# A hybrid decoder step on one core: another order of the filler blocks around the four chunks of a scan

## The chip, the cores and the metric

The kernel runs on one core of a Trainium2 chip. The metric is device time in microseconds (us) of one execution. The engines are named as in the profile: PE (TensorE, matmuls), ACT (ScalarE), DVE (VectorE), POOL (GpSimd), SP (SyncE, which issues most DMAs).

## The reference, cut to what matters

One decoder layer is computed for a prompt (512 tokens) and a sample group (8 requests of 4 tokens). Only the pieces that the change touches are shown: the modulation rows, the pooled cache rows, the input projection and the scan in four chunks of 128 tokens.

```python
def adaln_mods(c, w_ada, b_ada):
    m = (jax.nn.silu(c) @ w_ada + b_ada)[:, None, :]        # (1024) @ (1024, 6144)
    return jnp.split(m, 6, axis=-1)

def compress(rows, w_pos):                                   # pooled cache rows, 32 to 1
    b, l, g, d = rows.shape
    return jnp.einsum('bcjgd,j->bcgd', rows.reshape(b, l // CMP_BLOCK, CMP_BLOCK, g, d), w_pos)

rows = cache_cmp[layer, page_table].reshape(bd, PAST_LEN, 2, N_KV, HEAD_DIM)
kcmp = rmsnorm(compress(rows[:, :, 0], w_pos_k), g_k_cmp)
vcmp = compress(rows[:, :, 1], w_pos_v)

u = h @ w_in                                                 # (512+32, 1024) @ (1024, 2592)

def step(h, inp):                                            # one chunk of the scan
    xc, dtc, bc, cc = inp
    acs = jnp.cumsum(dtc * a, axis=1)
    seg = acs[:, :, None, :] - acs[:, None, :, :]
    decay = jnp.where(causal, jnp.exp(jnp.where(causal, seg, 0.0)), 0.0)
    cb = jnp.einsum('blhn,bshn->blsh', cc, bc)
    y_diag = jnp.einsum('blsh,bsh,bshp->blhp', cb * decay, dtc, xc)
    y_off = jnp.einsum('blhn,bhpn,blh->blhp', cc, h, jnp.exp(acs))
    w_end = jnp.exp(acs[:, -1:, :] - acs) * dtc
    h_new = jnp.exp(acs[:, -1])[:, :, None, None] * h + jnp.einsum('bsh,bshn,bshp->bhpn', w_end, bc, xc)
    return h_new, y_diag + y_off
```

## The kernel before

The program has three parts: projections and scan (up to about 258 us of the profile), attention, and the mixture of experts. The change touches the first part alone.

The steps of that part are written in an order given by the string `ORDER`. `C`, `z`, `q` and `B` are four projections of the normalised input by column blocks of `w_in` (weights wC, wF, wA, wB). Each splits its float32 weight into a high and a low part, k by k for the 8 blocks of 128 rows (`split_w`: ACT casts `wh` at L334, DVE subtracts `wl` at L335), and takes 12 products of 512 columns per k into four accumulators (tile `acc`); 16 small products per half of the weight are for the samples. Two pairs of wh and wl exist, so a projection's first two k can be split, and their 24 products issued, ahead of time. `c0` to `c3` are the four chunks of the scan (`ssd_chunk`), `p` prepares them, `e` finishes the state. A chunk is a chain over the engines: four transposes (L635), a copy of them (tile xt), small products with masks (UT, LT, ones), an exponential (L661, tile dec), a DVE product (L664), the products xt by dec, twice over for two groups of heads, then the state update (xdw by bt).

Between these stand sixteen filler blocks, which depend on none of them: eight `pool_batch` (pool0 to pool7; two 1 MB gathers from the paged cache, 32 products listed as 64) and eight `ada_block` (ada4 to ada11; a 1024 by 512 block of w_ada in two loads of 1 MB, 32 products listed as 64 and four with the bias listed as 8). They are taken in turn from one list: pool0, ada4, pool1, ada5 and so on to pool7, ada11.

```python
fillers = [f for n in range(8) for f in ((pool_batch, n), (ada_block, n + 4))]
...
BETWEEN = dict(C={3: (fill,), 6: (fill,)}, z={1: (fill,), 5: (fill,)}, q={1: (fill,), 5: (fill,)},
               B={1: (fill,), 3: (fill,), 5: (fill,)})
...
for step in ORDER.split():
    if step[0] == "f":
        fill(int(step[1:]))
    elif step[0] == "c":
        ssd_chunk(int(step[1:]))
    else:
        steps[step]()
```

One filler stands ahead of `ORDER`; a projection runs two or three between its k (after k=1, for instance); `f1` in `ORDER` runs one. What a filler and a projection put on PE is tied into one chain by `in_turn`, so PE takes those products in the order written. The chunks are outside that chain: a scheduler places their instructions among the others when the program is built, and on the chip every engine runs its instructions in that fixed order.

All big loads of the part (weights and gathers, 1 MB each) go through a ring of seven tiles (`SLOT`, pool `st`). A load waits until the tile that it is given has been read for the last time. SP's and POOL's queues are in order, so a load that waits holds up what is behind it.

Behind the part, attention begins with the transposes of the split queries (L913, tile qhl), which PE has right behind ada11; their copies (L100 on DVE, L102 on ACT, tile QT) follow a DVE chain that ends projection B (`k_side`, L563 to L568). The line of most matmuls is that of the helper, L92.

Of the kernel before, what the change touches and what calls it, by code (L numbers as in the profile page):

```python
# [22 lines left out]
TS = 4  # L23
NS = NB * TS
NE = 16
ORDER = "C p z c0 c1 q c2 f1 f1 c3 e B f1 f1 f1 f1"
WB = 6
XAT = 4
LA = 4
# [21 lines left out]
def hybrid_step(ctx: ExitStack, tc: tile.TileContext, a, o):  # L51
# [699 lines left out]
    steps = dict(C=proj_c, z=proj_z, p=ssd_prep, q=proj_q, B=proj_b, e=ssd_end)  # L751
    for step in ORDER.split():
        if step[0] == "f":
# [1422 lines left out]
```

## Time and profile before

| | |
|---|---|
| median of 3 runs | 783.35 us (783.32 to 785.89) |
| the profiled execution's own time | 787.62 us |
| its span, first to last instruction | 785.9 us |
| mean granted TensorE clock in it | 0.938 of full speed |
| PE busy | 709.3 us (90%) |
| DVE busy | 501.2 us (64%) |
| ACT busy | 355.2 us (45%) |
| POOL busy | 151.6 us (19%) |

Times in the trace are us from the span's start. An instruction's duration includes its pipeline, so durations overlap, and what a block costs in a row of blocks is the distance from its start to the next one's. A bracket behind a row is the idle time of its engine ahead of it and what ended that. PEclk is the granted clock of a stretch: 1.00 is 2.4 GHz, 0.50 is 1.2 GHz, and what lies between is a mixture.

### The profile page before, as it was taken

The page shows a single profiled execution, that of the slowest core. Times are in us where ns is not written, and L with a number is a line of the kernel's source. Part 1 is how long each engine was busy: PE and PEld are TensorE (multiplying, and loading weights), DVE is VectorE, ACT ScalarE, POOL GpSimd, SP SyncE. Part 2 cuts the span into 40 slices and gives each one's busy share as a digit, 9 for nine tenths or more (in the row PEclk, how much of TensorE's full clock was granted, in tenths as well). Part 3 has the DMA queues.
Part 4 walks back from the last instruction along what each step waited for, and adds up shares of the span by engine and source line. Part 5 has one row for each costly group of instructions (what it writes and reads, how often), then busy time and mean ns, then how long its engine had stood idle before and what let it go on. Part 6 is the DMA issues. An engine that isn't in the chain of part 4 may idle for free. (4 is left out here: it accounts for less than half of the span.)

```text
span 785.9 us, 14689 instructions
## 1 busy us (share of the span) xinstructions
PE 709.3 (90%) x5565; PEld 511.7 (65%) x5565; DVE 501.2 (64%) x1333; ACT 355.2 (45%) x813; POOL 151.6 (19%) x169
## 2 busy tenths in 40 slices
PE   4999999898999578998989999899668999999993
PEld 3667877676777355665647756687655766767562
DVE  5633692524644767554557555878986888877773
ACT  3423444515233333364434435613433766677661
POOL 1103012121321421010111200020131232233221
PEclk9999999889899879699999889999868999999997
DMA  8964895144559634423445041988767899997311
GB/s 286 355 187 131 289 330 193 58 162 161 214 191 346 253 143 172 149 81 134 164 158 219 2 108 23 360 267 286 290 253 282 270 333 335 334 329 256 86 25 23
DMA packets 67094, 161.86 MB, mean 206 GB/s; under 512 B 19005, under 2 KB 31238, under 8 KB 60622
## 3 DMA queue, kind: packets, MB, share of 16 engines
q1 hardware_dynamic: 56798, 115.54, 42.3%
q0 software_dynamic: 10224, 45.37, 17.5%
q8 instruction: 44, 0.72, 0.4%
q14 instruction: 28, 0.23, 0.1%
HBM read 153.48 MB, written 20.74 MB: 222 GB/s over the span
## 5 line engine op out<-in xcount | busy, mean ns | idle before, releaser
L92 PE MATMUL acc<-wh,hH 128*128 128x512 f32 (+1 forms) x128 | 48.9, 382 | 0.5 <-issue 0.5
L92 PE MATMUL acc<-wl,hH 128*128 128x512 f32 (+1 forms) x128 | 47.3, 370 | 0.0
L92 PE MATMUL acc<-wh,hL 128*128 128x512 f32 (+1 forms) x128 | 47.1, 368 | 0.0
L817 ACT ACTIVATE psb<-s,amx 128x128 f32<-128x128 f32 (+3 forms) x64 | 33.7, 528 | 27.4 <-DVE amx L815 24.3
L92 PE MATMUL acc<-gu,XF 128*128 128x512 f32 x88 | 46.1, 606 | 0.0
L92 PE MATMUL acc<-wh,XH 128*128 128x512 f32 x68 | 44.7, 657 | 0.4 <-ACT XH L1942 0.4
L815 DVE TENSOR_REDUCE amx<-s 128x1 f32<-128x128 f32 (+3 forms) x64 | 30.9, 484 | 17.3 <-PE s L92 17.3
L92 PE MATMUL ps<-wada,scT 128*32 128x128 f32 x768 | 38.0, 301 | 4.1 <-DMA wada<-in_w_ada 3.0
L92 PE MATMUL s<-KT,QT 128*128 128x384 f32 (+3 forms) x128 | 39.3, 392 | 1.3 <-DVE qa L838 0.8
L335 DVE TENSOR_TENSOR wl<-dn,wh 128x512 fp32r<-128x512 f32 x52 | 34.0, 686 | 7.0 <-ACT wh L334 6.9
L92 PEld LDWEIGHTS ps<-wada,scT 128*32 128x32 f32 x768 | 30.6, 122 | 10.3 <-issue 3.6
L1047 POOL DMA_INDIRECT gsel<-in_cache_sel,idx x16 | 20.6, 1289 | 84.3 <-PE smo L92 72.6
L334 ACT CAST wh<-dn 128x512 fp32r<-128x512 f32 x52 | 30.9, 619 | 12.9 <-PE acc L92 11.2
L820 PE MATMUL pt<-ident,psb 128*128 128x128 f32 x160 | 33.3, 308 | 3.3 <-ACT psb L817 3.3
L1991 POOL DMA_INDIRECT out_y_prompt<-yo,gi x13 | 21.4, 1646 | 74.8 <-DVE yo L1985 20.1
L335 DVE TENSOR_TENSOR wl<-gu,wh 128x512 fp32r<-128x512 f32 x44 | 29.5, 685 | 8.4 <-ACT wh L334 7.6
L92 PE MATMUL acc<-wh,HH 128*128 128x512 f32 x68 | 32.3, 478 | 1.6 <-ACT HH L1974 1.2
L334 ACT CAST wh<-gu 128x512 fp32r<-128x512 f32 x44 | 26.1, 619 | 15.8 <-PE acc L92 10.8
L92 PE MATMUL smo<-kt,Qb 128*32 128x512 f32 x80 | 29.6, 614 | 2.3 <-DVE kt L100 2.3
L102 ACT COPY kt<-sm 128x512 f32<-128x512 f32 x32 | 18.5, 584 | 27.6 <-PE sm L1023 24.0
L1985 DVE TENSOR_TENSOR yo<-acc,M 128x512 f32<-128x512 f32 x34 | 23.1, 686 | 11.5 <-PE acc L92 9.1
L92 PE MATMUL acc<-wl,HH 128*128 128x512 f32 x68 | 28.6, 421 | 0.0
(788 smaller groups left out, 1902.9 us busy)
## 6 DMA issues: line engine op xcount, KB each, us to landing
wada<-in_w_ada SPq DMA_DIRECT2D x24, 1024.0 KB
dn<-in_w_down SPq DMA_DIRECT2D x12, 1024.0 KB
gu<-in_w_gate SPq DMA_DIRECT2D x21, 512.0 KB
gu<-in_w_up SPq DMA_DIRECT2D x21, 512.0 KB
gux<-in_w_gate SPq DMA_DIRECT2D x11, 512.0 KB
gux<-in_w_up SPq DMA_DIRECT2D x11, 512.0 KB
wt<-in_cache_win SPq DMA_DIRECT2D x4, 1024.0 KB
wout<-in_w_out SPq DMA_DIRECT2D x4, 1024.0 KB
```

What stands on the lines that cost most here:

```text
L92: T.matmul(out, lhsT, rhs, start=start, stop=stop)
L102: S.copy(out, in_)
L334: S.copy(wh[:, 0:n], w)
L335: (eng or V).tensor_sub(wl[:, 0:n], w, wh[:, 0:n].bitcast(F32))
L815: V.tensor_reduce(mx, ps[:, 0:n], axis=AX.X, op=OP.max, negate=True)
L817: S.activation(pb[:, 0:n], ps[:, 0:n], AF.Exp, bias=mx, accum_out=sm[:, h:h + 1])
L820: T.transpose(pt[:, c * P:(c + 1) * P], pb[:, c * P:(c + 1) * P], ident)
L1047: G.indirect_dma_start(out=t.rearrange("p r c -> p (r c)"), out_offset=None, in_=sel_rows, in_offset=bass.IndirectOffsetOnAxis(ap=idx[:, 2 ...
L1985: V.tensor_tensor(yo[:, cols], po, M5[:, cols], op=OP.mult)
L1991: G.indirect_dma_start(out=y_p, out_offset=bass.IndirectOffsetOnAxis(ap=gi, axis=0), in_=yo, in_offset=None, bounds_check=511, oob_is_err= ...
```

## The change

The string that orders the steps is rewritten. Nothing else in the source changes, and the same sixteen fillers run.

```diff
-ORDER = "C p z c0 c1 q c2 f1 f1 c3 e B f1 f1 f1 f1"
+ORDER = "C p z c0 f1 c1 f1 q c2 f1 f1 c3 f1 e B f1"
```

| place | fillers before | fillers now |
|---|---|---|
| ahead, in C, in z | pool0; ada4, pool1; ada5, pool2 | the same |
| behind c0 | none | ada6 |
| behind c1 | none | pool3 |
| in q | ada6, pool3 | ada7, pool4 |
| behind c2 | ada7, pool4 | ada8, pool5 |
| behind c3 | none | ada9 |
| in B | ada8, pool5, ada9 | pool6, ada10, pool7 |
| behind B | pool6, ada10, pool7, ada11 | ada11 |

Since projection q is tied behind pool3 now, and projection B behind ada9, their products can no longer be placed among those of c1 and c3. PE's order shows it. The columns are line, operation, output and inputs, shape, and a count where equal instructions follow each other; wada is ada's weight, xx the conv output, wh, wl, hH and hL the parts of a projection's operands.

PE before, where c0 ends and c1 begins (first row: c0's state update; L635: c1's transposes):

```order
L92 MATMUL ps_1612<-xdw_1610,bt_1546 64x256 x2
L92 MATMUL ps_1557<-xt_1534,dec_1571 128x64
L635 MATMUL ps_1623<-ident,xx_815 128x128 x3
L92 MATMUL ps_1557<-xt_1534,dec_1571 128x64 x2
L635 MATMUL ps_1623<-ident,xx_815 128x128
L92 MATMUL acc_1724<-wh_1729,hH 128x512
L92 MATMUL acc_1724<-wl_1730,hH 128x512
L92 MATMUL acc_1724<-wh_1729,hL 128x512
```

PE now at the same place:

```order
L92 MATMUL ps_1612<-xdw_1610,bt_1546 64x256 x2
L92 MATMUL ps_1557<-xt_1534,dec_1571 128x64
L92 MATMUL ps_1626<-wada_1622,scT_89 32x128 x3
L92 MATMUL ps_1557<-xt_1534,dec_1571 128x64 x2
L92 MATMUL ps_1626<-wada_1622,scT_89 32x128 x13
L92 MATMUL ps_1581<-UT,lh_1588 128x128
L92 MATMUL ps_1626<-wada_1624,scT_89 32x128
L92 MATMUL ps_1581<-UT,lh_1591 128x128
L92 MATMUL ps_1626<-wada_1624,scT_89 32x128 x15
L92 MATMUL ps_1626<-bada_98,e_16_138 32x128 x4
L635 MATMUL ps_1665<-ident,xx_815 128x128 x4
L638 MATMUL ps_1671<-ident,xx_815 128x128
```

All 24 products of q's k=0 and k=1 stood among c1's rows; now ada6 stands at c0's end, c1's rows follow each other with nothing between, then come pool3 and those 24 products.

PE before, at the start of c3:

```order
L635 MATMUL ps_2187<-ident,xx_815 128x128 x4
L638 MATMUL ps_2193<-ident,xx_815 128x128
L92 MATMUL ps_2193<-dta_907,UT 128x8
L92 MATMUL ps_2193<-dta_907,LT 128x8
L92 MATMUL ps_2193<-dta_907,ones 128x8
L92 MATMUL ps_2203<-xx_815 128x128
L92 MATMUL acc_2317<-wh_2322,hH 128x512
L92 MATMUL acc_2317<-wl_2323,hH 128x512
```

PE now at the start of c3:

```order
L635 MATMUL ps_2267<-ident,xx_815 128x128 x4
L638 MATMUL ps_2273<-ident,xx_815 128x128
L92 MATMUL ps_2273<-dta_907,UT 128x8
L92 MATMUL ps_2273<-dta_907,LT 128x8
L92 MATMUL ps_2273<-dta_907,ones 128x8
L92 MATMUL ps_2283<-xx_815 128x128
L92 MATMUL ps_2286<-xx_815 128x128
L92 MATMUL ps_2290<-UT,lh_2291 128x128
L92 MATMUL ps_2290<-UT,lh_2294 128x128
```

Here too 24 products (B's k=0 and k=1) stood within the chunk; now they stand behind c3, ada9 and the state's transposes.

PE before, the end of the part (pool6, ada10 and pool7 stand ahead of the first row, behind B's last product):

```order
L92 MATMUL ps_2744<-gcmp_2742,PW_837 32x128
L92 MATMUL ps_2782<-wada_2778,scT_89 32x128 x16
L92 MATMUL ps_2782<-wada_2780,scT_89 32x128 x16
L92 MATMUL ps_2782<-bada_98,e_16_138 32x128 x4
L913 MATMUL s_2916<-ident,qhl_2913 128x128 x4
```

PE now, from B's last product on (x4k by Wp are B's own small products):

```order
L92 MATMUL acc_2442<-wh_2690,hL 128x512
L92 MATMUL ps_2730<-x4k_846,Wp_840 16x128
L92 MATMUL ps_2782<-wada_2778,scT_89 32x128 x10
L92 MATMUL ps_2730<-x4k_846,Wp_840 16x128
L92 MATMUL ps_2782<-wada_2778,scT_89 32x128 x2
L92 MATMUL ps_2730<-x4k_846,Wp_840 16x128
L92 MATMUL ps_2782<-wada_2778,scT_89 32x128 x4
L92 MATMUL ps_2782<-wada_2780,scT_89 32x128
L92 MATMUL ps_2730<-x4k_846,Wp_840 16x128 x5
L92 MATMUL ps_2782<-wada_2780,scT_89 32x128 x15
L92 MATMUL ps_2782<-bada_98,e_16_138 32x128 x4
L913 MATMUL s_2916<-ident,qhl_2913 128x128 x4
```

Of four blocks behind B one is left. The ring moves too: ada11's second load took the tile of pool6's first gather, which PE read behind B; now it takes that of wB's first half, which is read in the middle of B. wA's halves, which had tiles that came free during C and z, now take those of pool2's gathers; wB's first half, which had one that came free with pool3, now takes that of wA's second half.

On ACT, both of the early wB casts stand ahead of c2's last exponential (L661) now; before, one of them stood well ahead of it, in front of c2's first exponential.

## Rows read from the trace of the kernel before

**Rows 1.** The page's head: span and busy time.

```profile
span 785.9 us, 14689 instructions
PE 709.3 (90%) x5565; PEld 511.7 (65%) x5565; DVE 501.2 (64%) x1333; ACT 355.2 (45%) x813; POOL 151.6 (19%) x169
```

**Rows 2.** Busy time by stretch of the first part (us, each engine's busy time).

```profile
139.30:159.70 20.40, 17.62 (x101) 14.27 (x100) 10.78 (x25) 8.54 (x22) 3.74 (x3) 0.84 0.08 30
...
203.50:219.70 16.20, 13.98 (x87) 10.97 (x83) 9.97 (x26) 5.21 (x14) 3.40 (x4) 1.00 0.56 215
...
222.40:246.10 23.70, 23.61 (x276) 18.56 (x272) 5.78 (x19) 9.15 (x24) 5.18 (x6) 1.00 0.91 310
246.10:258.40 12.30, 9.87 (x289) 8.69 (x288) 7.72 (x26) 4.20 (x14) 2.04 (x7) 1.00 0.78 271
258.40:280.00 21.60, 12.29 (x77) 8.84 (x70) 20.10 (x68) 8.73 (x21) 11.51 (x19) 0.83 0.80 298
```

**Rows 3.** Timeline of PE, the end of c1 and ada6 (start, duration, ...).

```profile
151.87 0.43 PE L92 MATMUL ps<-xt,dec 128*128 128x64 f32 x2 [2.00 <-DVE dec L664]
152.14 0.66 PE L92 MATMUL ps<-UT,lh 128*128 128x128 f32 x4
...
159.67 3.64 PE L92 MATMUL ps<-wada,scT 128*32 128x128 f32 x64
163.24 0.51 PE L92 MATMUL ps<-bada,e 12*32 12x128 f32 x8
```

**Rows 4.** Windows of acc's products on PE: time, busy, count, granted clock.

```profile
163.70:169.30 5.60, 5.60 (x24) 1.00 0.98 345
```

**Rows 5.** Timeline of PE, the end of c3 and ada8.

```profile
211.92 0.61 PE L92 MATMUL ps<-UT,lh 128*128 128x128 f32 x4
213.96 0.43 PE L92 MATMUL ps<-xt,dec 128*128 128x64 f32 x2 [1.44 <-DVE dec L664]
214.24 0.66 PE L92 MATMUL ps<-UT,lh 128*128 128x128 f32 x4
...
219.15 0.60 PE L711 MATMUL ps<-ident,ST 128*64 128x128 f32 x4
220.16 1.96 PE L92 MATMUL ps<-wada,scT 128*32 128x128 f32 x64 [0.42 <-DVE ts L671]
```

**Rows 6.** PE by windows of 2 us: busy, count, granted clock, DMA.

```profile
152.00:154.00 2.00, 2.00 (x13) 0.81 0.00 0
...
162.00:164.00 2.00, 2.00 (x37) 0.63 0.54 103
...
192.00:194.00 2.00, 0.87 (x5) 1.00 0.00 1
194.00:196.00 2.00, 1.05 (x4) 0.55 0.00 0
...
212.00:214.00 2.00, 0.56 (x6) 1.00 0.40 157
```

**Rows 7.** Timeline of DVE at the start of c3.

```profile
204.06 2.50 DVE L734 TENSOR_TENSOR qa<-qa,rsq_zq 128x512 f32<-128x512 f32 x4
206.48 0.68 DVE L100 COPY xt<-ps 128x512 f32<-128x512 f32 x1
```

**Rows 8.** Timeline of PE: pool4 and ada11.

```profile
201.64 1.95 PE L92 MATMUL ps<-gcmp,PW 128*32 128x128 f32 x64
203.52 0.66 PE L635 MATMUL ps<-ident,xx 128*128 128x128 f32 x4
...
257.09 1.08 PE L92 MATMUL ps<-wada,scT 128*32 128x128 f32 x32 [2.43 <-DMA wada<-in_w_ada]
```

**Rows 9.** Timeline of DVE from B's last norm to the first QT copy.

```profile
251.78 0.76 DVE L568 TENSOR_TENSOR selo<-selo,rsq_zk 128x256 f32<-128x256 f32 x2
...
259.58 0.69 DVE L100 CAST QT<-s 128x512 fp32r<-128x512 f32 x1 [4.36 <-PE s L913]
```

**Rows 10.** Timeline of ACT in c2.

```profile
186.14 0.62 ACT L334 CAST wh<-wB 128x512 fp32r<-128x512 f32 x1 [2.26 <-DMA wB<-in_w_in]
...
194.21 0.60 ACT L661 ACTIVATE dec<-ps 128x512 f32<-128x512 f32 x1
```

## The prediction

> **What bounds the kernel now.** I read the page's head first. PE is busy 709.3 of 785.9 us [rows 1], so PE's own work and its idle time make the time; no block is dropped, and a gain can only come from PE's waits or its clock. Then the windows, stretch by stretch. In c1 (139.30 to 159.70) PE is idle for 2.8 us, in c3 (203.50 to 219.70) for 2.2, in B for 0.1, and behind B (246.10 to 258.40) for 2.4. From 258.40 on DVE is the bound, with 20.10 of 21.60 us [rows 2]. The timeline shows the waits: 2.00 us at 151.87 and 1.44 at 213.96, both for dec of DVE [rows 3, 5], and 2.43 at 257.09 for ada11's second load [rows 8]. DVE begins attention's copies at 259.58 after 4.36 us of idle time, though its own chain of B ended at 252.54 [rows 9]. The windows of 2 us show the clock: it falls in 152:154, after c1's wait, and returns in 162:164; it falls again in 194:196, after c2's waits; in c3 it stays at 1.00 [rows 6].
>
> What must be compared is therefore the stretch from c0's end (139.3) to DVE's first QT copy (259.6): 120.3 us. Ahead of it the two orders are the same, and behind it too.
>
> **Before, in five pieces.** (1) c1, 24 products of q, ada6: 139.3 to 163.7, 24.4 us [rows 2, 4]. (2) The rest of q, c2, ada7, pool4: 163.7 to 203.5, 39.8 us [rows 4, 8]. (3) c3, 24 products of B, the state's transposes, ada8: to 222.4, 18.9 us [rows 2, 5]. (4) B's other 72 products and its samples, pool5, ada9: to 246.1, 23.7 us [rows 2]. (5) pool6, ada10, pool7, ada11 and the way to the QT copy: 13.5 us [rows 2, 9].
>
> **Prices.** 24 products of 512 columns take 5.6 us [rows 4]. A pool block takes 1.9 us (201.64 to 203.52) [rows 8]. An ada block takes 2.24 us at 2.4 GHz (220.16 to 222.4) [rows 2, 5], but ada6, which met the lower clock, took 4.0 (159.67 to 163.7) [rows 3, 4]: 1.8 more. The second half of a chunk took 4.91 us at full clock in c3 (214.24 to 219.15) [rows 5] and 7.53 in c1 (152.14 to 159.67) [rows 3]: 2.6 more. A chunk that loses the clock at its middle thus costs 2.6 + 1.8 = 4.4 us with the block behind it.
>
> **The change, piece by piece, at full clock.**
>
> *Piece 1.* ada6 moves ahead of c1, pool3 and ada7 come behind it, and q's 24 products leave c1's rows for a place behind pool3. c1 alone: the stretch of 20.4 us, less 5.6 for the products, less 2.6 since it ran half at the lower clock: 12.2 us. This takes it that the products covered none of c1's waits; had they covered waits all along, c1 alone would keep 17.8. I take 12.2, since PE was idle only 2.8 of the 20.4 us: the products were mostly work to be done, not cover. Sum: 12.2 + 5.6 + ada6 2.24 + pool3 1.88 + ada7 2.24 = 24.2, against 24.4.
>
> *Piece 2.* It has a block of each kind one number on, at the same price. wB's first half now takes the tile of wA's second half, which PE reads to the end of q (about 186), so it lands later than before, when a cast at 186.14 already waited 2.26 us for it [rows 10]. Both early casts and a scaling now stand ahead of c2's last exponential (194.21 [rows 10]): two casts of 0.6 and a wait. wA's halves, too, come later now, behind pool2's reads, and hold ACT a little in q. Hidden if ACT has slack, at most the 2.26 of the wait seen; I take 1.0: 40.8.
>
> *Piece 3.* B's 24 products leave c3, and ada9 comes behind it. c3 alone, step by step: its xt copy ends 3.6 us after its transposes start (203.52 [rows 8], 206.48 + 0.68 [rows 7]), because DVE works at L734 until then; some 1.9 us of short steps follow (an estimate: copies of 0.7 and small products of 0.6, as in these rows); then 7.2 us from the last group's UT products at 211.92 to the transposes of the state at 219.15 [rows 5]. That is 12.7, between 10.05 (219.15 - 203.5 less 5.6: products never cover) and 15.65 (they always do). Sum: 12.7 + ada9 2.24 + 0.42 for the wait ahead of it [rows 5] + 0.6 transposes + 5.6 = 21.5, against 18.9; the ada block that ended the piece is still in it.
>
> *Piece 4.* Three blocks instead of two: 23.7 + 1.9 = 25.6. Their DVE and ACT copies have room (5.78 and 9.15 of 23.7 us [rows 2]).
>
> *Piece 5.* One ada block remains and stands among B's last products, with its loads into tiles that are free long before, so the 2.43 us of waiting go. What is left is the DVE chain: 252.54 - 246.1 = 6.4, and 0.2 to the copy; ada11's 2.24 us lie beneath it. 6.6 against 13.5. Were that chain not the bound, the floor is about 3 us (ada11 and the transposes); were the samples' work to delay it, 8.
>
> Sum: 24.2 + 40.8 + 21.5 + 25.6 + 6.6 = 118.7 against 120.3, **-1.6 us** at full clock. The tail gives 6.9, and 5.3 goes back, since blocks that stood behind B must run somewhere.
>
> The loads that are issued earlier don't collide: the DMA share is 0.00 where c1 and c2 wait [rows 6]. SP's and POOL's queues keep the order of their loads with the blocks; each block's tiles come free at least a chunk ahead of its use. What a late one costs is shown by ada11: 2.43 [rows 8].
>
> **Why the blocks do not fill the chunks' waits.** PE idled 2.00 us at 151.87 [rows 3], though ada6's products, whose loads had landed (DMA share 0.00 there [rows 6]), came next but for c1's own rows. A block behind a chunk runs behind it. The Trainium skill says so too ("TensorE: Matmul & The Clock Gate", Step-by-step: what each phase is for): matmuls stay in program order, and only weight loads are pulled ahead; the trace agrees. What did fill waits before, 24 products each in c1 and in c3, is what the change takes out.
>
> **The clock.** c1 and c3 now run bare from end to end, as only the last part of each did. c1 before fell after one wait of 2.00; c2 after 0.67 and 1.41 with a few products between (PE busy 0.87 and 1.05 of two times 2 us); c3 stood 1.44 and stayed at 1.00 [rows 3, 5, 6]. Bare c3 has a wait of over 2 us at its start (copy at 206.48, behind L734) and further ones of about 1.3 and 1.1, so I expect it to fall, like c1 before. Bare c1 has no L734 ahead of its copy; its waits, about 1.3 and 1.4 with products between, look like c3's tail, and I expect it to hold, with little margin. One fall is +4.4.
>
> **Forecast.** One of the two chunks, likelier c3, drops to 1.2 GHz: -1.6 + 4.4 = **+2.8 us**. The profiled execution took 787.62 us, 4.3 over the median of 783.35; I add the difference to both: 790.4 for a profile like it, and 786.1 at the median.
>
> **Rivals.**
> - *Both fall (slower).* c1's bare waits are long enough as well. For it speaks c2, which fell on no more; against it c3's tail. -1.6 + 8.8 = +7.2: 790.5. It decides whether PEclk drops in the middle of c1.
> - *Neither falls (faster).* The blocks just ahead of c1 and c3 keep PE busy until the chunk, and the waits stay short: -1.6, 781.8; with the tail at its floor or c3 at its lower bound, down to 779. The Trainium skill's rule ("TensorE: Matmul & The Clock Gate", What's actually happening) is that the clock falls after an idle stretch and that sustained work brings it back; chunks with products between their waits might hold by it, and the sum would be this one. Against it stands c2 at 0.55 in 194:196 after waits of 0.67 and 1.41 [rows 6].
> - *The blocks do cover the waits.* PE would get back the 2.0 and 1.4 us of waiting and the clock besides (4.4), with the tail's gain: -6 to -8, about 776. The order speaks against it: no block's row stands within c1 or c3.
> - *Bare chunks are much longer* (17.8 and 15.65, the upper bounds): about +8 over the sum at full clock, and a fall is then near certain: 793 or more. PE's idle time of 2.8 and 2.2 us before speaks against it.
>
> **How the numbers follow.** One falls 0.44, both 0.26, neither 0.17, the blocks cover 0.05, long chunks 0.08. The time predicted is 786.1. 0.5% of 783.35 is 3.9 us, about what a measurement of this kernel can tell from no change: faster is under 779.4, slower over 787.3. Faster holds the cover case and half of neither, whose bounds reach below: 0.14. Slower holds both, long chunks, and a small part of one-falls, whose piece 2 may cost 1.3 more: 0.38. The same: 0.48. The range runs from 780 to 791: below it lies the cover case and a little of neither, above it the long chunks and a little of both. The likeliest case's own range is 784 to 788.
>
> **What the changed profile would show.** Piece 5 is right if DVE's first QT copy comes within 7 us of B's last product, with no DMA wait at ada11. Piece 1: c1 from transposes to pool3 in 12 us, PEclk 1.00 throughout. Piece 3: a wait of 2 to 3 us behind c3's transposes, PEclk 0.5 in c3's second half, ada9 at nearly 4 us. Piece 2: ACT waits for wB ahead of c2's last exponential. The prediction is wrong if c3 keeps 1.00, if c1 loses it, or if PE waits for a DMA at ada6, pool3 or ada9.

## The result: slower by 0.9%, and the profile after

| | before | after |
|---|---|---|
| median, measured together | 785.89 us (9 runs) | 792.33 us (9 runs) |
| ratio, 95% interval | | 1.0091 (1.0062 to 1.0121) |
| profiled execution, own time | 787.62 us | 797.4 us |
| its span | 785.9 us | 795.7 us |

The ratio is 7 us of 786, beside a forecast of +2.8. It is the number of the rival in which both chunks lose the clock (+7.2). The time itself, 792.33 us, lies above the forecast 786.1 and its range to 791; 2.5 us of that is the kernel before, which was 783.35 us when the forecast was added to it and 785.89 here. Executions more than 1.5% above the fastest of their kernel (two of the kernel before, one of the kernel with a block within c1 and c3) are left out of the ratios.

The page's head after, beside [rows 1]: PE is busy 7.3 us longer with the same 5565 matmuls, so they ran slower.

```profile
span 795.7 us, 14695 instructions
PE 716.6 (90%) x5565; PEld 517.8 (65%) x5565; DVE 502.1 (63%) x1333; ACT 355.9 (45%) x813; POOL 150.3 (19%) x169
```

PE by windows of 2 us after, beside [rows 6] (time, busy, count, granted clock, DMA share, GB/s). The first group is c1 and pool3, the second c2's end, the third c3 and ada9.

```profile
146.00:148.00 2.00, 2.00 (x15) 1.00 1.04 303
148.00:150.00 2.00, 1.94 (x9) 0.57 0.93 393
150.00:152.00 2.00, 0.78 (x4) 0.50 0.05 21
...
164.00:166.00 2.00, 2.00 (x13) 0.66 0.25 26
...
202.00:204.00 2.00, 0.00 (x0) 0.73 0.00 0
...
216.00:218.00 2.00, 1.34 (x6) 0.64 0.96 389
218.00:220.00 2.00, 1.26 (x6) 0.50 1.08 440
...
230.00:232.00 2.00, 2.00 (x42) 0.95 0.47 109
```

c1 falls to 1.2 GHz at about 148, 3 us after its first row, and returns at about 165. Before, it fell 14 us after its first row (139.25 to 153) and was back after 10. c3, which held 1.00 before, is at 0.50 from about 217 to 230. c2 falls as it did before.

PE's timeline after, c1 (beside [rows 3]).

```profile
140.49 0.42 PE L92 MATMUL ps<-wada,scT 128*32 128x128 f32 x6
...
144.94 0.66 PE L635 MATMUL ps<-ident,xx 128*128 128x128 f32 x4
...
151.79 0.69 PE L92 MATMUL ps<-xt,dec 128*128 128x64 f32 x2 [1.22 <-DVE dec L664]
...
157.80 1.12 PE L92 MATMUL ps<-xdw,bt 128*64 128x256 f32 x4 [0.78 <-ACT dec L661]
...
160.75 3.64 PE L92 MATMUL ps<-gcmp,PW 128*32 128x128 f32 x64
164.32 0.80 PE L92 MATMUL acc<-wh,hH 128*128 128x512 f32 x1
```

The waits named are short, 1.22 and 0.78, and the clock had fallen before the first of them began (150.57). The loss is in what runs: pool3 takes 3.57 us (160.75 to 164.32) where a pool block at full clock took 1.9 [rows 8].

PE's timeline after, c3 and what follows (beside [rows 5]).

```profile
212.53 0.66 PE L635 MATMUL ps<-ident,xx 128*128 128x128 f32 x4
...
215.44 0.71 PE L92 MATMUL ps<-UT,lh 128*128 128x128 f32 x4 [1.05 <-DVE xt L100]
...
218.74 0.69 PE L92 MATMUL ps<-xt,dec 128*128 128x64 f32 x2 [1.07 <-DVE dec L664]
...
227.71 3.15 PE L92 MATMUL ps<-wada,scT 128*32 128x128 f32 x64
230.78 0.42 PE L92 MATMUL ps<-bada,e 12*32 12x128 f32 x8
```

DVE's timeline after, from B's last norm to the first QT copy (beside [rows 9]).

```profile
268.05 0.78 DVE L568 TENSOR_TENSOR selo<-selo,rsq_zk 128x256 f32<-128x256 f32 x2
...
269.03 0.67 DVE L100 CAST QT<-s 128x512 fp32r<-128x512 f32 x1
```

DVE no longer waits for PE there: the 4.36 us of idle time are gone, and the tail does what was forecast. The row behind B's last product starts at 262.3, and the copy came 6.7 us after that.

### The profile page after: what moved, and what is told of

The parts are those of the page before. It is cut to its first block, busy times and chain, and to the rows that moved or that the text cites. A ratio compares the mean times of both kernels' runs of the same rounds, so it can differ in the third digit from the quotient of the medians.

```text
span 795.7 us, 14695 instructions
## 1 busy us (share of the span) xinstructions
PE 716.6 (90%) x5565; PEld 517.8 (65%) x5565; DVE 502.1 (63%) x1333; ACT 355.9 (45%) x813; POOL 150.3 (19%) x169
## 5 line engine op out<-in xcount | busy, mean ns | idle before, releaser
L92 PE MATMUL ps<-wada,scT 128*32 128x128 f32 x768 | 39.7, 299 | 0.6 <-DVE rsq_yxs L113 0.3
L92 PE MATMUL s<-KT,QT 128*128 128x384 f32 (+3 forms) x128 | 37.6, 379 | 2.2 <-DVE qa L838 1.2
L820 PE MATMUL pt<-ident,psb 128*128 128x128 f32 x160 | 31.1, 295 | 1.8 <-ACT psb L817 1.4
L504 POOL DMA_INDIRECT gcmp<-in_cache_cmp,idx x16 | 16.8, 1051 | 79.0 <-PE ps L92 62.2
L92 PE MATMUL acc<-wl,XH 128*128 128x512 f32 x68 | 28.9, 425 | 1.9 <-DVE wl L335 1.9
```

The source lines that it names most:

```text
L92: T.matmul(out, lhsT, rhs, start=start, stop=stop)
L504: G.indirect_dma_start(out=gt.rearrange("p r c -> p (r c)"), out_offset=None, in_=cmp_rows, in_offset=bass.IndirectOffsetOnAxis(ap=idx[:, ...
L820: T.transpose(pt[:, c * P:(c + 1) * P], pb[:, c * P:(c + 1) * P], ident)
```

## The experiments

The stretch of a kernel below is from c0's last state update (xdw by bt) to DVE's first QT copy. "At 1.2 GHz" is 2 x (1 - PEclk) x length. "Filled" means that the projection's 24 products stand among the chunk's rows, "bare" that they don't. A time is a ratio to the kernel before, run in the same rounds; the second number of the first line is the kernel before against itself, built again.

| kernel | c1 | c3 | stretch us | at 1.2 GHz us | ratio (interval) |
|---|---|---|---|---|---|
| before, two profiles | filled | filled | 121.2, 120.0 | 17, 17 | 1; 0.9968 (0.9937 to 1.0000) |
| after, two profiles | bare | bare | 129.5, 128.3 | 36, 33 | 1.0091; 1.0083 (1.005 to 1.0115) |
| only c1's blocks new | bare | filled | 122.4 | 20 | 1.0044 (1.0011 to 1.0076) |
| only c3's block new | filled | bare | 121.0 | 19 | 1.0088 (1.005 to 1.0126) |
| both mended | filled | filled | 119.1 | 7 | 0.9954 (0.9918 to 0.9989) |
| c1 mended, two profiles | filled | bare | 124.7, 125.1 | 20, 20 | 1.0222 (1.0169 to 1.0276); 1.0163 (1.0096 to 1.0229) |
| c3 mended | bare | filled | 124.9 | 20 | 1.0077 (1.005 to 1.0104) |
| 34 extra products | bare, but for them | bare, but for them | 125.7 | 8 | 1.0098 (1.0063 to 1.0132) |
| a block within c1 and c3 | block | block, part of B | 117.5 | 9 | 1.0017 (0.9981 to 1.0053) |
| two behind B | filled | filled | 124.3 | 27 | 0.9999 (0.9961 to 1.0037) |
| three behind B | filled | filled | 113.5 | 5 | 0.9961 (0.9928 to 0.9994) |

**Which place costs.** Each of the two places alone.

```diff
-ORDER = "C p z c0 f1 c1 f1 q c2 f1 f1 c3 f1 e B f1"
+ORDER = "C p z c0 f1 c1 f1 q c2 f1 f1 c3 e B f1 f1"
```

> The new places behind c0 and c1 are kept (ada6, pool3), but nothing is put behind c3; two blocks stay behind B. The profile after the change showed the piece with c1 longer by 7.8 us, the piece with c3 by 5.8, B by 1.4, and the tail shorter by 6.8. Clock theory (a chunk that runs without the projection's products loses the clock): c1 at 1.2 GHz, c3 at 1.00 as before; +7.8 for c1, the tail shorter by 4 to 6, the third block in B paid already: 1 to 4 us above the kernel before. Rival, late loads or the tail are at fault and not c1: within 1 us of the kernel before or faster.

```diff
-ORDER = "C p z c0 f1 c1 f1 q c2 f1 f1 c3 f1 e B f1"
+ORDER = "C p z c0 c1 q c2 f1 f1 c3 f1 e B f1 f1 f1"
```

> c0, c1 and q are those of the kernel before; only the block behind c3 is new, and three stay behind B. Clock theory: c1 as before (falls after its wait of 2 us), c3 bare and at 1.2 GHz in its second half; +5.8 for c3, the tail shorter by 2 to 4.6: 1 to 4 us above the kernel before. Rival, c3 alone doesn't lose the clock (its fall needs what c1's change left behind): the block costs 2.2 and the tail gives it back, within 1 us of the kernel before.

With c1's blocks alone the kernel is 3.5 us above before, c1 at 1.2 GHz from about 151 to 164, c3 at 1.00: the clocks are as the clock theory had them. That the time fits too is in part luck. By stages, against the means of the two profiles of before, its profile is 1.8 us longer in the stretch, 1.6 shorter in attention and 3.7 longer in the mixture of experts. PE by windows, one from c1 and one from c3:

```profile
152.00:154.00 2.00, 2.00 (x9) 0.50 0.02 4
...
221.00:222.00 1.00, 0.33 (x3) 1.00 0.04 16
```

With c3's block alone c3 falls from 203 to 220, but the time is 7 us above, nearly twice the upper end of what was expected. In that profiled execution (785.93 us, the fastest of its twelve) c1, whose rows are those of before, held the clock; nine of the twelve took 791.8 to 797.4, with a mean granted clock of 0.919 to 0.929 against 0.934 to 0.936 in the other three. No profile shows where those nine lose their time. Windows of c1 and c3 in this kernel:

```profile
154.00:156.00 2.00, 1.28 (x10) 1.00 0.00 0
...
208.00:209.00 1.00, 1.00 (x5) 0.50 0.45 182
```

Both kernels are slower than before by their times; in the stretch they are 1.8 and 0.4 us longer.

**The same blocks and tiles, ahead of the chunks.** Everything is as in the changed kernel, the ring of loads included, but no block stands right behind c1 or c3.

```diff
-ORDER = "C p z c0 f1 c1 f1 q c2 f1 f1 c3 f1 e B f1"
+ORDER = "C p z c0 f1 f1 c1 q c2 f1 f1 f1 c3 e B f1"
```

> The same blocks, the same tiles of the ring and one block behind B as in the changed kernel, but the two blocks around c1 both stand ahead of it, and the one behind c3 stands ahead of it, so that the 24 products of q and of B can be placed among the rows of c1 and c3 again. Clock theory, and the theory that the bare chains' length is the loss: c1 and c3 as long as before the change, the tail 6.9 us shorter, the three moved blocks 6.0 at full clock: 0 to 3 us below the kernel before, 7 to 10 below the changed one. Rival, the loads that come later (wA, wB, the ring) are the loss: as slow as the changed kernel, 5 to 9 us above the kernel before.

782.72 us, 0.9954: 3.6 us below before and some 10 below the changed kernel. (The kernel before measured 0.9968 against itself, so a gain over it is not shown; the 10 us are clear of that.) Late loads fall as a theory, since these are the same loads in the same tiles; nor does PE wait for a DMA in the stretch in either profile after the change. The windows of c1 in this kernel: waits, and no fall.

```profile
156.00:158.00 2.00, 1.44 (x9) 1.00 0.00 0
158.00:160.00 2.00, 1.12 (x8) 1.00 0.00 0
160.00:162.00 2.00, 1.76 (x14) 1.00 0.01 4
162.00:164.00 2.00, 1.40 (x11) 1.00 0.00 0
164.00:166.00 2.00, 2.00 (x67) 1.00 0.03 8
```

**One chunk mended at a time,** with the changed kernel again in the same rounds.

```diff
-ORDER = "C p z c0 f1 c1 f1 q c2 f1 f1 c3 f1 e B f1"
+ORDER = "C p z c0 f1 f1 c1 q c2 f1 f1 c3 f1 e B f1"
```

```diff
-ORDER = "C p z c0 f1 c1 f1 q c2 f1 f1 c3 f1 e B f1"
+ORDER = "C p z c0 f1 c1 f1 q c2 f1 f1 f1 c3 e B f1"
```

> The changed kernel once more, on the chip and in the rounds of the next three, so that they can be compared with it: 5 to 9 us above the kernel before, as measured at first. Its second profile also shows what varies from one execution to the next: if the clock in c1 or c3 holds this time, the fall depends on the execution, not on the order alone.

> Only c1 is mended: pool3 stands with ada6 ahead of c1, so that q's products lie within it; c3 is bare, as in the changed kernel. Two causes, c1 bare and c3 bare, as in the pieces of the traces (2.3 and 2.4 us at full clock, and half clock in both): about half of the 9.6 us between the changed kernel and the one with both mended, so 4 to 6 us below the changed kernel. If c1 alone is the cause: 8 to 10 below; if c3 alone: within 2.

> Only c3 is mended: ada9 stands ahead of c3, so that B's products lie within it; c1 is bare, as in the changed kernel. Two causes: 4 to 6 us below the changed kernel. If c1 alone is the cause: within 2; if c3 alone: 8 to 10 below.

The changed kernel took 790.85 us (1.0083), as at first, and both c1 and c3 fell again. In the stretch the two causes nearly add up: 128.9 with both bare (mean of two), 124.9 with c1 filled, 124.9 with c3 filled, 119.1 with both filled, and 35, 20, 20 and 7 us at 1.2 GHz. Whole windows (time, PE busy, clock) of the second profile after the change, stretch, attention and the rest,

```profile
137.89:266.15 128.26, 118.72 (x1288) 0.87 0.47 166
266.15:492.00 225.85, 201.67 (x1672) 0.95 0.42 148
492.00:787.10 295.10, 264.12 (x1380) 0.94 0.72 243
```

and of the kernel with c1 mended:

```profile
139.42:264.14 124.72, 115.86 (x1288) 0.92 0.50 170
264.14:499.14 235.00, 209.68 (x1672) 0.91 0.40 142
499.14:795.10 295.96, 263.58 (x1380) 0.93 0.72 242
```

PE's idle time in the stretch is 9.5 and 8.9 us; the difference is in its busy time. But the times of the whole runs contradict the expectation of 4 to 6 us below the changed kernel for each: c1 mended took 799.59 us, 9 above it by the medians, and c3 mended 789.96, within 1, which was the forecast for c1 as the only cause. With c1 mended the stretch gains 3.5 and attention gives back 9.2 (235.00 against 225.85, at 0.91 against 0.95); against the first profile after the change it is 4.8 and 6.0.

> The kernel with only c1 mended again, since it measured 799.6 us though its stretch up to the first QT copy took only 124.7 (after the change 128 to 129). If the clock behind that stretch is what costs, this look shows more time at 1.2 GHz in attention or in the mixture of experts than the 76 us of its first profile; if it is something else (a load, an engine), the same clock and a longer wait.

It did so again: 798.1 us, stretch 125.1, attention 235.5 at 0.91, so it belongs to that kernel. The rest of the program was at 0.93 both times. Beside the kernel before (means of two profiles each) it is 4.3 us longer in the stretch, 2.5 in attention and 3.3 in the mixture of experts. Attention in the kernel with c1's blocks alone, whose order of instructions there is almost the same, took 231.2 at 0.93. What makes its waits come so that the clock falls more often is open.

**Work instead of waits.** The changed kernel with seventeen products of 512 columns in each of c1 and c3.

```diff
             pseg = PS()
+            if c in (1, 3):
+                for k in range(4):
+                    mm(pseg, hH[:, k, 0:P], hL[:, k, 0:512])
...
+            if c in (1, 3) and g == 0:
+                for k in range(5):
+                    mm(py, hH[:, k, 0:P], hL[:, k, 0:512])
...
         pst = PS()
+        if c in (1, 3):
+            for k in range(4):
+                mm(pst, hH[:, k, 0:P], hL[:, k, 0:512])
```

> The changed kernel, and in c1 and c3 seventeen extra products of 512 columns each, written into sums that the chunk's own products then overwrite: 34 products of 0.227 us, 7.7 us of PE's time, part of it in waits. It keeps the order and the bare chain but gives PE work. Clock theory: PEclk 1.00 through c1 and c3, their pieces shorter by about 7.6 us at full clock, less 2 to 5 us of products that no wait hides: 3 to 6 us below the changed kernel, 1 to 5 above the kernel before. Length theory (the bare chain is what costs, at either clock): no gain, 0 to 8 us above the changed kernel.

The trace shows the mechanism, the time doesn't bear it out. c1 holds the clock, in the same order of the chunk's own work:

```profile
146.00:148.00 2.00, 2.00 (x11) 1.00 0.95 397
148.00:150.00 2.00, 2.00 (x10) 1.00 0.13 53
150.00:152.00 2.00, 1.73 (x9) 1.00 0.00 0
...
156.00:158.00 2.00, 2.00 (x18) 1.00 0.00 0
```

From c1's transposes to pool3 it is 14.8 us with 3.9 us of products in it, against 15.8 without them, and pool3 takes 1.9 again. The stretch is 3.2 us shorter than after (125.70 against the mean of 128.9). Yet the median is 794.52 us, as slow as the changed kernel: what was expected by the length theory, not 3 to 6 us below it as by the clock theory. Part of what the clock gave was spent on products that the result doesn't need, and in this execution, with 790.17 us the fastest of nine, attention took 233.2 at 0.90, longer than in either profile of the changed kernel. Against the length theory stands the trace, in which the same chain is shorter with more work in it; the time does not confirm that, and by its time alone the experiment decides nothing for the clock.

**The rival made true: a block within the chunk.**

```diff
             S.activation(dec, pseg.rearrange("p (i l) -> p i l", l=P), AF.Exp)
+            if c in (1, 3) and g == 0:
+                fill()
...
-ORDER = "C p z c0 f1 c1 f1 q c2 f1 f1 c3 f1 e B f1"
+ORDER = "C p z c0 c1 f1 q c2 f1 f1 c3 e B f1"
```

> The rival that the blocks cover the chunk's waits, made true: ada6 and ada9 are put into c1 and c3 themselves, behind the first exponential, where PE waited for DVE's dec; one block stays behind B. If what matters is that PE has work in the chunk, and any work will do: the waits of 1.2 to 2 us are covered, 4 to 8 us below the changed kernel, near the kernel before. If one block is too little, or its order delays the chunk's own products: within 2 us of the changed kernel.

786.34 us: near the kernel before, some 5 below the changed one (1.0017 against 1.0083 in the same rounds). c3 falls for some 3 us only; c1 holds 1.00, with ada6 where the wait for dec was:

```profile
143.59 0.86 PE L92 MATMUL ps<-wada,scT 128*32 128x128 f32 x24
144.39 0.49 PE L92 MATMUL ps<-UT,lh 128*128 128x128 f32 x2
144.81 1.30 PE L92 MATMUL ps<-wada,scT 128*32 128x128 f32 x40
146.03 0.42 PE L92 MATMUL ps<-bada,e 12*32 12x128 f32 x8
146.38 0.43 PE L92 MATMUL ps<-xt,dec 128*128 128x64 f32 x2
```

The stretch of 117.5 us is 3 below before. A block does cover a chunk's wait, if it stands in it; the change put none there.

**Two versions drawn from this, and the kernel before again.**

```diff
-ORDER = "C p z c0 f1 c1 f1 q c2 f1 f1 c3 f1 e B f1"
+ORDER = "C p z c0 f1 c1 q c2 f1 f1 f1 c3 e B f1 f1"
```

```diff
-ORDER = "C p z c0 f1 c1 f1 q c2 f1 f1 c3 f1 e B f1"
+ORDER = "C p z c0 f1 c1 q c2 f1 f1 c3 e B f1 f1 f1"
```

> A version drawn from the runs: one block (ada6) ahead of c1, three ahead of c3, none right behind them, and two behind B, since DVE's chain behind B takes 6.4 us and two blocks 4.1. From c0's last state update to the first QT copy 119 us or less, against 121.2 before; half-clock time in it below 17 us. Time 1 to 4 us below the kernel before, as the one with both chunks filled, or up to 2 lower than that.

> The smallest step from the kernel before: only ada6 moves, from q to a place ahead of c1, and three blocks stay behind B. The wait of 2.43 us for ada11's load should go, and ada6 runs at full clock: 1 to 4 us below the kernel before. If the tail of three blocks (6.0 us and B's samples) is longer than DVE's chain, 2 us more.

> The kernel before once more, for a second profile of the same order. If the clock's falls belong to the order, c1 falls and c3 holds again, and attention has again some 38 us at 1.2 GHz. If they depend on the execution, these differ while the order is the same.

With two behind B nothing is gained (786.15 us): c1 fell at about 157 and c3 at 222, though both are filled. Its stretch is 124.3 us where 119 or less was expected, in a profiled execution of 789.84 us, the second slowest of twelve. With three behind B it is 783.15 us, 0.9961, and the shortest stretch of all, 113.5 at 0.98, in an execution of 779.28 us, the second fastest of twelve; the wait for ada11's load is gone, though the first QT copy comes 9 us after B's last product, since three blocks and B's samples outlast DVE's chain. That it is faster than the kernel before is not shown: in the same rounds the kernel before, built again, took 783.32 us (0.9968). Its c1, with nearly the same waits as the other's, held. The rows of the two at c1, first two behind B:

```profile
152.00:154.00 2.00, 1.56 (x9) 1.00 0.00 0
154.00:156.00 2.00, 1.00 (x8) 1.00 0.00 0
156.00:158.00 2.00, 2.00 (x13) 0.77 0.02 4
158.00:160.00 2.00, 1.22 (x7) 0.50 0.00 0
```

```profile
152.00:154.00 2.00, 1.78 (x10) 1.00 0.00 0
154.00:156.00 2.00, 0.78 (x6) 1.00 0.00 0
156.00:158.00 2.00, 2.00 (x16) 1.00 0.01 4
158.00:160.00 2.00, 1.16 (x9) 1.00 0.00 0
```

In the second profile of the kernel before, c1 fell at about 151 and c3 held, as at first; attention had 37 us at 1.2 GHz (231.2 at 0.92), near the 38 expected. The fall in c1 is thus not certain with that order: it came in these two profiles, while the kernel with c3's block alone has the same rows there and held.

## Why the prediction was wrong, point by point

By its own five pieces, with the profile after:

| piece | forecast at full clock | measured | where |
|---|---|---|---|
| 1 | 24.2 | 32.2 | 140.5 to 172.7 |
| 2 | 40.8 | 39.8 | to 212.5 |
| 3 | 21.5 (25.9 with a fall) | 24.7 | to 237.2 |
| 4 | 25.6 | 25.1 | to 262.3 |
| 5 | 6.6 | 6.7 | to 269.0 |
| sum | 118.7 (123.1) | 128.5 | before: 120.3 |

**The step that failed** is "Bare c1 has no L734 ahead of its copy; its waits, about 1.3 and 1.4 with products between, look like c3's tail, and I expect it to hold, with little margin". Bare c1 fell in all four profiles that have it without extra products (after, twice; c1's blocks alone; c3 mended). The waits were mis-sized to begin with: the one for dec of DVE is 1.91 us in three of the four, near the 2.00 of c1 before, and the one behind it 0.78. But waits are not all of it. In the first profile after the change (three windows of 1 us) the clock fell at 148.3 while PE counts as busy throughout, from 140.5 on with small products alone, and c1's first named wait began at 150.57:

```profile
145.00:146.00 1.00, 1.00 (x12) 1.00 1.04 406
...
147.00:148.00 1.00, 1.00 (x8) 1.00 0.90 199
148.00:149.00 1.00, 1.00 (x6) 0.65 0.93 393
```

In the second profile it fell within the wait for dec:

```profile
148.00:150.00 2.00, 0.23 (x2) 0.70 0.13 53
...
150.14 0.69 PE L92 MATMUL ps<-xt,dec 128*128 128x64 f32 x2 [1.91 <-DVE dec L664]
```

Comparing single waits with single waits was the error, as far as these runs show: c3's tail held after a stretch of B's products, bare c1 has only small products from its first row on, and with seventeen products of 512 columns among its rows it held. Filled c1 with a block ahead held in four profiles of five.

**A fall priced too low, and rows that moved, in piece 1.** It is 8.0 us too long. Of these, 5.8 are the clock: 3.6 in c1 itself (15.8 from transposes to pool3 against 12.2), 1.7 in pool3 at half clock, 0.5 in the first products. A fall was priced at 4.4 since it was taken to come in the middle of the chunk; here it came 3 us after c1's start. The other 2.2 are in ada6, whose 2.24 us became 4.45 (140.49 to 144.94), because c0's last UT, lh and xt, dec products, which ran among c1's transposes and q's products before, now stand with it. The forecast had counted these rows within its 12.2, so c1 without them was taken a little too short. At full clock c1 without them takes about 12.2 (an estimate): with c1's blocks alone, the half that ran at 1.00 took 7.3 (143.79 to 151.12), and c3's second half 4.91 [rows 5]. (c0's last eight products xt by dec still stand among c1's rows, at 146.13 and 147.12, so these do not quite follow each other with nothing between.)

**Piece 3 was right in kind and size:** c3 fell in all six profiles that have it bare (in the sixth, with extra products, for 3 us only), ada9 took 3.4 us, and the wait for xt behind L734 is there, 1.05 us of it as idle time. 24.7 against 25.9.

**Piece 2** cost nothing in sum (39.8 as before), where 1.0 was taken. The mechanism is there: ACT waits for wB (0.59) and casts both halves ahead of c2's last exponential, now at 203.53, and PE's wait behind it is one of 2.67, where there were two of 0.67 and 1.41.

**Pieces 4 and 5 were right.** The tail's gain of 6.8 us is real, and it went where the sum said, into the blocks' new places.

**Where the gain went.** In the stretch, 128.9 against 120.6 (means of two): +8.3. PE is idle for 9.5 to 9.6 us in it after and 9.2 to 10.0 before, so the loss is not idle time but longer busy time; at 1.2 GHz it is 35 us against 17. Attention took 229.0 and 225.9 where it took 234.3 and 231.2: -5.3. The rest took 297.7 and 295.1 against 292.0 and 294.5: +3.1. With 0.8 ahead of the stretch that is +6.9, beside the 7.1 of the ratio. The sentence that the order behind the stretch is the same was wrong: the scheduler put attention's instructions, and those of the mixture of experts, in another order too. In attention, whether that or chance gave the 5.3 is open: two kernels with nearly the order of before there (c3's block alone, three behind B) took 230.1 and 228.9, and one with the changed kernel's order (two behind B) 228.5. In the mixture of experts the +3.1 goes with the order: the six profiles with the changed kernel's order (its own two, c1's blocks alone, c1 mended twice, two behind B) took 295.1 to 297.7, the three with that of before (its own two, c3's block alone) 292.0 to 294.5. What in that order costs is not shown.

**The rivals.** "Both fall" is what happened, at 0.26; its price, 8.8, was made of 2.6 and 1.8 for each chunk, and mending both chunks gave 9.8 in the stretch. That the whole time met its +7.2 is in part luck: the stretch alone is +8.3, and the other stages, which no rival touched, add -5.3, +3.1 and +0.8. "The blocks do cover the waits" was rightly argued from the order to be false here, and could have been true of another order. The Trainium skill's rule on matmuls in program order (TensorE: Matmul & The Clock Gate, Step-by-step: what each phase is for) agrees with the traces after the change: no row of pool3, the block behind c1, came into c1's waits of 1.22 and 0.78. The Trainium skill's rule that the clock falls after idle time and returns with work (the same page, What's actually happening) agrees with the runs only in part: c1 held with extra products in its waits, and the second profile after the change fell in a wait, but the first fell at 148.3 with PE counted as busy.

## What to carry to other kernels

Independent work that is tied into one order has two prices: where it runs, and what it pushes out. Here blocks behind a latency-bound chain pushed out the products that had kept TensorE busy within it, and the chain and the block behind it ran at half clock. Put such work ahead of the chain or inside its waits, keep the wide products among its rows, and leave at the end what another engine's chain hides anyway (here 6.4 us of DVE: from the start of B's last product the first QT copy came 7.0 us later with one block behind B in the changed kernel, 7.2 and 7.6 with two, 9.4 with three). In the stretch this paid in three of the four kernels that did it for both chunks (117.5, 119.1 and 113.5 us against 120.6, but 124.3 with two behind B); in the whole time none of them is shown to be faster than the kernel before.

## What the runs showed that was not expected

One order of instructions does not have one clock. The same c1 fell in two profiles of the kernel before and held in another kernel with the same rows; the stretch at 25 to 30 us, untouched by any change, was at 0.66 to 0.69 in four of the profiles and at 1.00 in the others. Over 84 executions of the kernel before, run beside the experiments, the time ran from 778.1 us (mean granted clock 0.951) to 790.2 (0.930): median 782.7 with a clock of 0.942 or more (31 executions), 787.0 from 0.936 to 0.942 (38), 789.0 below (15). A straight line through them gives 0.32 us of time per us at 1.2 GHz. By it, the changed kernel's 12.5 us more at 1.2 GHz (mean of its 19 executions against those 84) are 4.0 of the 6.5 us between the two means; the other 2.5 don't follow the mean clock.

A gain in one stage came back as a loss in another stage with no common work: against the changed kernel, the one with c1 mended gained 4 us in the stretch and lost some 8 in attention (means of two profiles each), where its instructions also stand in another order. In this program a stage's own windows told what an edit did there, and only the whole time, over many runs, whether it was worth it.
